# 64-byte places of two operands in a retention/GLA layer: sums of x in pairs, four of seven weight products shifted, a small tile ahead of the heads' output

## The chip, the core and the metric

The kernel runs on one core of a Trainium2 chip. TensorE (PE) multiplies, VectorE (DVE), ScalarE (ACT) and GpSimd (POOL) do the elementwise work, SyncE (SP) and POOL issue DMAs. The metric is the device time of one execution in microseconds; lower is better.

## The reference, cut to what matters

One layer with two branches over 512 positions and 16 meta positions, model width 1024:

```python
u = rms_norm(h, norm_gain)                       # (528, 1024)
(rq, rk, rv, rg, gq, gk, gv, gg, glr, m_ret, m_gla) = split(u @ w_in)
o_ret = head_group_norm(retention(rope(rq), rope(rk) / 16, rv)) * silu(rg)   # 4 heads, 256 -> 512
o_gla = head_rms_norm(gla(gq, gk, gv, log_sigmoid(glr @ w_gate_up + b_gate) / 16)) * silu(gg)
merged = sigmoid(m_ret) * (o_ret @ w_branch_ret) + sigmoid(m_gla) * (o_gla @ w_branch_gla)
out = rms_norm(h + merged @ w_out, final_norm_gain)[16:]
```

All is float32. The kernel splits each float32 operand into a rounded high part (hi) and the rest (lo), both float32r, and forms a product from three matmuls: hi x hi, hi x lo, lo x hi.

## The kernel before

Most of the time goes to `quad`, which multiplies x (two halves of 256 positions, th, by two halves of 512 rows, kh) by a block of 512 weight columns with seven block products in place of eight. The products are numbered 1, 2, 6, 7, 5, 4, 3 in the order they run. Products 1, 2 and 4 take a block of x itself (the names A11, A12 for the first half of positions, A22 for the second); 5, 6, 7 and 3 take sums of blocks, S1, S2, S3, S4, that `form` makes once. A list `fh` holds the seven high parts and `fl` the seven low parts. One product has 24 matmuls: two column halves t, four row blocks kk, and the three of hi and lo.

- In quads with `rows=True` (gg, gv, rg, rv) the weights' 256 columns stream as the moving operand and 128 positions of x are the stationary one. In mr, mg, rqk and gqk it is the other way round: 128 weight columns are stationary, and x's 256 or 264 positions stream.
- bg and wo1 use `quad` too, with lists of their own in place of fh and fl (`forms`).
- `wsplit` gives the tiles for hi and lo of the next weights (three buffers each); ScalarE casts to hi and VectorE subtracts for lo (`split`, line 154). The matmuls of the quads are line 318.
- `branch` and `ret_branches` multiply a head's turned output oh, ol (four row blocks by 512 positions, moving) by w_branch_ret (stationary, 128 columns), with `mm3` (lines 189 to 193); this is br. oh and ol of heads 0 to 2 are in the pool rp, those of head 3 take the place of x in the pool cp.

The order on each engine follows the code, with a pin that keeps the matmuls of a product together. `weave` mixes the quads with the chains of attention and gates. Weights come by SP's DMAs; the sums of two weight blocks come by DMAs from POOL that accumulate (line 282).

A tile's place in SBUF is a byte address within each partition, the same for all partitions. From the built program's memory map, modulo 128 bytes, before the change:

| operand | step from row block to row block | place modulo 128 |
|---|---|---|
| x, first half (A11, A12) | 2 x 272 x 4 = 2176 = 17 x 128 | 64 |
| x, second half (A22) | 2176 | 64 + 1088 = 0 |
| S1 to S4, one tile each, `[P, 4, 272]` | 272 x 4 = 1088 = 8.5 x 128 | 64, 0, 64, 0 |
| weights hi, lo, all products | 256 x 4 = 1024 | 64 |
| oh, ol of heads 0 to 2 | 2048 | 0 |
| oh, ol of head 3 | 2048 | 64 |

Of the kernel before, what the change touches and what calls it, by code (L numbers as in the profile page):

```python
# [21 lines left out]
F32 = mybir.dt.float32  # L22
F32R = mybir.dt.float32r
# [5 lines left out]
P = 128  # L29
D = 1024  # L30
T = 512
NM = 16
# [14 lines left out]
SOFF = (0, 512, 896, 1152)  # L47
E_U, E_D, E_A, E_B, E_END, E_ND = range(6)
A11, A12, A22, S1, S2, S3, S4 = range(7)


def constants():
# [56 lines left out]
def hybrid_kernel(ctx: ExitStack, tc: tile.TileContext, I, out: bass.AP):  # L109
# [22 lines left out]
    al = {(th, kh): xl[kh][:, :, th] for th in range(2) for kh in range(2)}  # L132
    fh = [ah[0, 0], ah[0, 1], ah[1, 1]]
    fl = [al[0, 0], al[0, 1], al[1, 1]]
    fh += [cp.tile([P, 4, HW], F32R, tag=f"fh{i}", name=f"fh{i}") for i in range(3, 7)]
    fl += [cp.tile([P, 4, HW], F32R, tag=f"fl{i}", name=f"fl{i}") for i in range(3, 7)]

    rt = cp.tile([P, NTB + 1], F32, name="rt")
    rneg = cp.tile([P, NTB + 1], F32, name="rneg")
    rb = cp.tile([P, 2, HT], F32, name="rb")  # L140
    um = cp.tile([P, KD, 32], F32, name="um")
    sel = cp.tile([P, P], F32R, name="sel")
    rgain = cp.tile([P, 16], F32, name="rgain")
    ggain = cp.tile([P, 8], F32, name="ggain")
# [50 lines left out]
            order[:] = [m]  # L195

    def rstd_of(x, n, rows, name, eps=EPS):
        v = sp.tile([P, 1], F32, tag="rv", name=f"{name}_v")
        r = sp.tile([P, 1], F32, tag="rr", name=f"{name}_r")
        nc.vector.tensor_scalar(v[:rows], x, 1.0 / n, eps, op0=ALU.mult, op1=ALU.add)  # L200
        R["pow"] = nc.gpsimd.tensor_tensor(r[:rows], v[:rows], mhalf[:rows], op=ALU.pow)
        return r
# [45 lines left out]
    def wraw(name, shape=(P, 4, 256)):  # L248
        return wp.tile(list(shape), F32, tag="raw", name=name, bufs=6)

    def wsplit(shape, name):
        return (wp.tile(shape, F32R, tag="whi", name=f"{name}_h", bufs=3),
                wp.tile(shape, F32R, tag="wlo", name=f"{name}_l", bufs=3))

    low = []

    def quad(cols, rows, name, evac, meta=None, adds=True, ahead=False, behind=None, src=None,
# [42 lines left out]
            return form[kk // 2][:, kk % 2] if isinstance(form, list) else form[:, kk]  # L300

        def prepare(i, w):
            hi, lo = wsplit([P, 4, 256], f"{name}_{i}")
            low[:] = split(hi, lo, w)
            return hi, lo

# [33 lines left out]
        if meta is not None:  # L340
            psm = pat(f"{name}_pm")
            for n in range(2):
                for kh in range(2):
                    for g in range(4):
                        nc.tensor.matmul(psm[32 * g:32 * g + 32, n * 256:(n + 1) * 256], um[:, 4 * kh + g, :],
                                         (w11, w21)[kh][:, g, :] if n == 0 else (w12, w22)[kh][:, g, :], start=n == 0 and kh == 0, stop=kh == 1,
                                         skip_group_check=n > 0)
        product(1, A11, w11, b, True)
# [223 lines left out]
    wps = pat("warm_p")  # L572
    for _ in range(10):
        nc.tensor.matmul(wps, wzero[:, :P], wzero, start=True, stop=True)
    nc.gpsimd.memset(um, 0.0)
    nc.gpsimd.tensor_copy(sel, selr)
    nc.gpsimd.memset(ones, 1.0)

# [9 lines left out]
    def small_rows():  # L588

        for k in range(KD):  # L590
            g = k % 4
            m = nc.tensor.matmul(psm[32 * g:32 * g + 32], um[:, k, :], graw[k // 2][:, k % 2, :],
                                 start=k < 4, stop=k >= 4)
            if k == 0:
                pin(m)
        for s in range(2):
            for k in range(KD):
                g = k % 4
                m = nc.tensor.matmul(glr[s][32 * g:32 * g + 32, :HT], wl[:, k, :], u[k // 4][:, k % 4, s],
                                     start=k < 4, stop=k >= 4)  # L600
        order[:] = [m]

    for q in range(4):
        raw = graw[q]
        hi, lo = wsplit([P, 2, 512], f"gv0_{q}")
        for kk in range(2):
            kh, k = divmod(2 * q + kk, 4)
            g = ng[:, 2 * q + kk:2 * q + kk + 1]
            cast = nc.scalar.activation(xh[kh][:, k, :, :HT], u[kh][:, k], AF.Copy, scale=g)
            casts.append(cast)  # L610
            if k == kh == 0:
                nc.vector.tensor_copy(hi[:, kk, :], raw[:, kk, :])
                w = nc.vector.tensor_sub(lo[:, kk, :], raw[:, kk, :], hi[:, kk, :].bitcast(F32))
            x = nc.vector.scalar_tensor_tensor(xl[kh][:, k, :, :HT], u[kh][:, k], g, xh[kh][:, k, :, :HT].bitcast(F32),
                                               op0=ALU.mult, op1=ALU.subtract)
            if k == kh == 0:
                after(x, w)
            if k or kh:
                split(hi[:, kk, :], lo[:, kk, :], raw[:, kk, :])

        if q == 3:
            for kh in range(2):
                for k in range(4):
                    x = nc.scalar.activation(u[kh][:, k], u[kh][:, k], AF.Copy, scale=ng[:, 4 * kh + k:4 * kh + k + 1])
                    if kh == 1:
                        act(x)
                    else:
                        after(x, casts[-1])
                x = nc.vector.tensor_copy(um[:, 4 * kh:4 * kh + 4, :NM].rearrange("p k (h m) -> p k h m", h=2),
                                          u[kh][:, :, :, 256:HT])  # L630
                if kh == 1:
                    vec(x)
            small_rows()
        steps = [(t, kk, j) for t in range(NTB) for kk in range(2) for j in range(3)]
        if q < 3:
            steps.sort(key=(lambda x: (x[1], -x[2] % 3 if x[1] == 0 else x[2])) if q < 2 else (lambda x: x[1]))
        for t, kk, j in steps:
            kh, k = divmod(2 * q + kk, 4)
            c = slice((t % 2) * P, (t % 2 + 1) * P)
            m = nc.tensor.matmul(pss[t], (al if j == 1 else ah)[t // 2, kh][:, k, c], (lo if j == 2 else hi)[:, kk, :],  # L640
                                 start=q == kk == j == 0, stop=q == 3 and kk == 1 and j == 2)
            pin(m)
            order[:] = [m]
# [241 lines left out]
    def gla_attention(p):  # L885
# [14 lines left out]
        def decays(b):  # L900
            lah, lal = split_la(b, P)
            for h in range(2):
# [11 lines left out]
                G["exp"] = nc.scalar.activation(X[:, 2:5, :], pf[:, :384].rearrange("p (e t) -> p e t", e=3), AF.Exp)  # L914
                Q[b, h] = gp.tile([P, 4, P], F32, tag="gQ", name=f"gQ{n}", bufs=4)
                K[b, h] = gp.tile([P, 4, P], F32, tag="gK", name=f"gK{n}", bufs=2)
                TO[b, h] = sp.tile([P, 1], F32, tag="gto", name=f"gto{n}")
                qb = q[:, h, b * P:(b + 1) * P].unsqueeze(1).to_broadcast([P, 4, P])
                kb = k[:, h, b // 2, (b % 2) * P:(b % 2 + 1) * P].unsqueeze(1).to_broadcast([P, 4, P])
                nc.vector.tensor_mul(K[b, h], X[:, 2:6, :], kb)  # L920
# [405 lines left out]
    def ret_attention(h):  # L1326
        sh, sl, sm = R["s", h]
        vh, vl = R["v", h]
        vm, sg = R["vm", h], R["sg", h]

        oh, ol = [(rp if h < 3 else cp).tile([P, 4, T], F32R, tag=f"o{n}" if h < 3 else f"x{n}0", name=f"o{n}{h}")
                  for n in "hl"]
        R["o", h] = oh, ol

        def values(ib):
            ps = pat(f"av{h}{ib}")
            for jb in range(ib + 1):
                o = SOFF[jb] + (ib - jb) * P
                mm3(ps, sh[:, o:o + P], sl[:, o:o + P], vh[:, jb, :], vl[:, jb, :], jb == 0, False)
            nc.tensor.matmul(ps, sm[:, ib * P:(ib + 1) * P], vm, start=False, stop=True)  # L1340
            b6 = sp.tile([P, 6], F32, tag="b6", name=f"b6{h}{ib}")
            mv = sp.tile([P, 2], F32, tag="mv", name=f"mv{h}{ib}")
            nc.vector.bn_stats(b6, ps)
            nc.vector.bn_aggr(mv, b6)
            r = rstd_of(mv[:, 1:2], 1.0, P, f"g{h}{ib}")
            nm = sp.tile([P, 1], F32, tag="nm", name=f"nm{h}{ib}")
            nc.vector.scalar_tensor_tensor(nm, mv[:, 0:1], -1.0, r, op0=ALU.mult, op1=ALU.mult)  # L1347
            on = tmp(f"on{h}{ib}")
            nc.scalar.activation(on, ps, AF.Identity, scale=r, bias=nm)  # L1349
            nc.vector.tensor_mul(sg[:, ib, :], on, sg[:, ib, :])  # L1350

        for ib in range(NTB):
            values(ib)
            R["pow", h] = R["pow"]
            yield
        if h < 2:
            yield
        for half in range(2):
            turn(sg, half, oh, ol, rgain, h * 4, f"ot{h}")
            yield  # L1360
# [82 lines left out]
    for h in range(4):  # L1443
# [10 lines left out]
        else:  # L1454
# [2 lines left out]

    mh, ml = [[cp.tile([P, 4, T], F32R, tag=f"x{n}1", name=f"m{n}0"),
               rp.tile([P, 4, T], F32R, tag=("sg", "vl")[n == "l"], name=f"m{n}1")] for n in "hl"]
    sums = [[cp.tile([P, 4, 256], F32R, tag=f"f{n}{i}", name=f"ms{n}{i}") for i in range(3, 7)] for n in "hl"]  # L1460
    mforms = [[m[0][:, :, :256], m[1][:, :, :256], m[1][:, :, 256:], *x] for m, x in zip((mh, ml), sums)]

    def merged(k, t):
# [43 lines left out]
    def square(t, o):  # L1507
# [4 lines left out]
        if o == 768:  # L1512
            nc.vector.tensor_tensor_reduce(sq[:, :256], hh, hh, 1.0 / D, vs[t], ALU.mult, ALU.add, v)
        else:
            ss = sp.tile([P, 1], F32, tag="ss", name=f"fss{t}{o}")
            nc.scalar.activation(sq[:, :256], hh, AF.Square, accum_out=ss)
            nc.gpsimd.tensor_scalar(v, ss, 1.0 / D, vs.get(t, EPS), op0=ALU.mult, op1=ALU.add)
        vs[t] = v
# [1 line left out]
            nc.gpsimd.tensor_mul(hh, hh, fgb[:, o:o + 256])  # L1520
        if o < 768:
            return
        r = sp.tile([P, 1], F32, tag="rr", name=f"fr{t}")
        nc.gpsimd.tensor_tensor(r, v, mhalf, op=ALU.pow)
        h0, h1 = hs[0][:, t, :], hs[1][:, t, :]
        nc.scalar.activation(h0, h0, AF.Copy, scale=r)
# [82 lines left out]
```

## Time and profile before

| | |
|---|---|
| time, median of 3 runs | 761.6 us (761.6 to 762.16) |
| profiled execution | 761.8 us, of it the span 760.0 us |
| TensorE busy | 749.8 us (99%), 5595 matmuls |
| VectorE busy | 611.4 us (80%) |
| ScalarE busy | 450.8 us (59%) |
| GpSimd busy | 141.9 us (19%) |
| granted TensorE clock, mean over the span | 0.997 |
| DMA | 116.89 MB, mean 154 GB/s |

A matmul's record runs from its start to the modelled end of its way through the array, so neighbours overlap; how long a matmul holds the array is seen from start to start, or from a group that spans many of them. In the view by stretches a row gives the stretch, its length, then for PE, PEld, DVE, ACT and POOL the busy time and the count of instructions in it, then the granted clock, the DMA share and GB/s. In the chain a row gives start, length and what ran. In the timeline a row gives start, length, engine, line, operation, out<-in, shape and count, and in brackets idle time ahead of it.

### The profile page before, as it was taken

To read this page: it belongs to the slowest core of one execution; us is meant where nothing else is said; L and a number is where in the kernel's file an instruction comes from. 1 tells how busy PE (TensorE), PEld (TensorE's weight loads), DVE (VectorE), ACT (ScalarE), POOL (GpSimd) and SP (SyncE) were. 2 spreads that over 40 slices of the span, in tenths; PEclk is the share of its full clock that TensorE was granted. 3 is DMA by queue.
4 is the path that set the end of the run, shared out by engine and by line. 5 is a ranking of instruction groups with operands and counts; after the bars stand their busy time and mean duration, and the time that the engine had idled before them with its cause. 6 is when DMAs were issued, how large, how long until landed. Compare 5 with 4: busy or idle time off the path is not lost.

```text
span 760.0 us, 14059 instructions
## 1 busy us (share of the span) xinstructions
PE 749.8 (99%) x5595; PEld 701.8 (92%) x5595; DVE 611.4 (80%) x873; ACT 450.8 (59%) x764; POOL 141.9 (19%) x172
## 2 busy tenths in 40 slices
PE   9999999999989999999999999999999999999996
PEld 6799899999989999999989999989999999988996
DVE  6799878689897789789957688966787989775994
ACT  7897584666974566546546555646464756532562
POOL 2211200112231122110530100440011210111142
PEclk9999999999999999999999999999999999999999
DMA  9864321822568972733783562794476356687503
GB/s 301 287 138 100 95 85 43 184 82 65 145 157 232 303 170 88 173 111 130 200 245 119 120 158 86 203 238 119 131 165 144 109 141 193 229 191 201 131 29 112
DMA packets 99994, 116.89 MB, mean 154 GB/s; under 512 B 5716, under 2 KB 90836, under 8 KB 99672
## 3 DMA queue, kind: packets, MB, share of 16 engines
q1 hardware_dynamic: 79896, 88.19, 36.7%
q0 software_dynamic: 19744, 27.27, 19.7%
q8 instruction: 44, 0.72, 0.4%
q10 hardware_dynamic: 288, 0.53, 0.2%
q14 instruction: 22, 0.18, 0.1%
HBM read 104.44 MB, written 11.53 MB: 153 GB/s over the span
## 4 chain that ended last, share of the span: by engine, by line
PE 91%; DVE 6%; issue 2%; ACT 1%; POOL 0%; POOLq 0%; DVEq 0%
PE rqk_b L318 6%; PE rv_b L318 6%; PE rg_b L318 6%; PE rqk_c L318 5%; PE br_p L189 4%; PE br_p L193 4%; PE br_p L192 4%; PE gg_b L318 3%; PE mr_b L318 3%; PE mg_b L318 3%; PE gv_p L640 3%; PE rv_c L318 3%; PE bg_b L318 3%; PE rg_c L318 3%; PE gg_c L318 2%
## 5 line engine op out<-in xcount | busy, mean ns | idle before, releaser
L189 PE MATMUL br_p<-oh,br_h 128*128 128x512 f32 x128 | 50.4, 394 | 0.0
L192 PE MATMUL br_p<-ol,br_h 128*128 128x512 f32 x128 | 50.4, 393 | 0.0
L193 PE MATMUL br_p<-oh,br_l 128*128 128x512 f32 x128 | 50.4, 393 | 0.0
L154 ACT CAST rv_h<-rv_w 128x1024 fp32r<-128x1024 f32 x24 | 25.3, 1052 | 27.1 <-DVE rv_w L371 9.6
L154 DVE TENSOR_TENSOR rv_l<-rv_w,rv_h 128x1024 fp32r<-128x1024 f32 x24 | 29.3, 1222 | 9.2 <-ACT rv_h L154 9.2
L154 DVE TENSOR_TENSOR rg_l<-rg_w,rg_h 128x1024 fp32r<-128x1024 f32 x20 | 24.4, 1222 | 8.7 <-ACT rg_h L154 8.7
L282 POOL DMA_DIRECT2D rqk_x<-in_w_in_dram x8 | 10.4, 1302 | 108.0 <-DVE rv_l L154 80.6
L154 ACT CAST rg_h<-rg_w 128x1024 fp32r<-128x1024 f32 x20 | 21.0, 1051 | 15.8 <-PE br_p L192 6.2
L193 PEld LDWEIGHTS br_p<-oh,br_l 128*128 128x128 f32 x128 | 24.0, 188 | 5.7
L189 PEld LDWEIGHTS br_p<-oh,br_h 128*128 128x128 f32 x128 | 24.0, 188 | 5.0
L192 PEld LDWEIGHTS br_p<-ol,br_h 128*128 128x128 f32 x128 | 24.0, 188 | 5.0
L154 ACT CAST br_h<-br_w 128x1024 fp32r<-128x1024 f32 x16 | 16.8, 1049 | 19.2 <-PE br_p L192 9.9
L154 ACT CAST rqk_h<-rqk_w 128x1024 fp32r<-128x1024 f32 x20 | 21.0, 1052 | 11.6 <-PE rqk_c L318 2.9
L1349 ACT ACTIVATE on<-av,nm,g_r 128x512 f32<-128x512 f32 x16 | 12.5, 780 | 25.4 <-DVE nm L1347 25.4
L318 PE MATMUL rv_b<-rv_l,fh 128*128 128x256 f32 x96 | 27.1, 282 | 0.2 <-DVE rv_l L154 0.2
L318 PE MATMUL rqk_b<-fh,rqk_h 128*128 128x256 f32 (+1 forms) x96 | 27.2, 283 | 0.0
L318 PE MATMUL rqk_b<-fh,rqk_l 128*128 128x256 f32 (+1 forms) x96 | 27.1, 283 | 0.0
L318 PE MATMUL rqk_b<-fl,rqk_h 128*128 128x256 f32 (+1 forms) x96 | 27.1, 282 | 0.0
L318 PE MATMUL rg_b<-rg_h,fl 128*128 128x256 f32 x96 | 27.0, 281 | 0.0
L154 DVE TENSOR_TENSOR rqk_l<-rqk_w,rqk_h 128x1024 fp32r<-128x1024 f32 x20 | 24.4, 1220 | 3.2 <-ACT rqk_h L154 3.2
L318 PE MATMUL rv_b<-rv_h,fl 128*128 128x256 f32 x96 | 27.0, 281 | 0.0
L318 PE MATMUL rg_b<-rg_h,fh 128*128 128x256 f32 x96 | 26.9, 281 | 0.0
(720 smaller groups left out, 3266.6 us busy)
## 6 DMA issues: line engine op xcount, KB each, us to landing
rv_w<-in_w_in_dram SPq DMA_DIRECT2D x16, 512.0 KB, 4.1
br_w<-in_w_branch_ret_dram SPq DMA_DIRECT2D x16, 512.0 KB, 3.4
rqk_w<-in_w_in_dram SPq DMA_DIRECT2D x12, 512.0 KB, 4.8
rg_w<-in_w_in_dram SPq DMA_DIRECT2D x12, 512.0 KB, 4.9
rqk_x<-in_w_in_dram SPq DMA_DIRECT2D x8, 512.0 KB, 3.9
rqk_x<-in_w_in_dram POOLq DMA_DIRECT2D x8, 512.0 KB, 8.2
rg_x<-in_w_in_dram SPq DMA_DIRECT2D x8, 512.0 KB, 3.7
rg_x<-in_w_in_dram POOLq DMA_DIRECT2D x8, 512.0 KB, 7.7
```

The source lines that it names most:

```text
L154: return nc.scalar.copy(hi, src), nc.vector.tensor_sub(lo, src, hi.bitcast(F32))
L189: m = nc.tensor.matmul(o, lh, rh, start=first, stop=False)
L192: nc.tensor.matmul(o, lh, rl, start=False, stop=False)
L193: m = nc.tensor.matmul(o, ll, rh, start=False, stop=last)
L282: x = nc.gpsimd.dma_start(t, block(0, 1), accum_op=ALU.add)
L318: m = nc.tensor.matmul(ps[t][:, :n] if wide else ps[t], l, r, start=first and j == 0, stop=kk == 3 and j == 2, skip_group_check=not fresh ...
L640: m = nc.tensor.matmul(pss[t], (al if j == 1 else ah)[t // 2, kh][:, k, c], (lo if j == 2 else hi)[:, kk, :], start=q == kk == j == 0, sto ...
L1349: nc.scalar.activation(on, ps, AF.Identity, scale=r, bias=nm)
```

## The change

1. S1 and S2 share one tile `[P, 4, 2, 272]` with row blocks interleaved, S3 and S4 another, so that a form's step from row block to row block is 2176, as in x. S1 and S3 then lie at 64, S2 and S4 at 0 modulo 128 for all kk. The sums in the output product (`sums`) use the same two tiles, as two `[P, 4, 256]` halves.
2. `wsplit` makes its tiles 32 elements (128 bytes) longer, so that the three buffers lie 4224 bytes apart. With `odd` the weights start 64 bytes into the tile; otherwise 0 or 128 bytes, by turns that follow the buffers' rotation. `odd` is set for products 1, 2, 5 and 7 of the quads on fh.
3. A memset of a 64-byte tile, `gap`, on POOL ahead of head 0's oh: oh and ol of heads 0 to 2 move from 0 to 64 modulo 128.
4. Room for it: statistics tiles (rv, rr, gto, b6, mv, nm, ss) have 3 or 4 buffers in place of 5, and um (x of the meta positions) is one tile of 160 columns in which eight windows of 32 columns overlap by 16. The second 16 columns of a window, zero before, now hold the next block's values; they reach rows of a sum that nothing reads.

With it, the reads of a matmul's moving operand and of the stationary operand that is loaded beside it lie 64 bytes apart modulo 128 in all products of the 20 quads on fh (products 1 and 2 before: 0; product 4: 64; the S products: 0 and 64 by turns). For br of heads 0 to 2 it goes from 64 to 0. Modulo 256, hi and lo of the odd products lie 128 bytes apart; in the others, at one place, except where buffers don't come in turn (72 of the 288 matmuls of br).

```diff
 A11, A12, A22, S1, S2, S3, S4 = range(7)
+ODD = (1, 2, 5, 7)
...
-    fh += [cp.tile([P, 4, HW], F32R, tag=f"fh{i}", name=f"fh{i}") for i in range(3, 7)]
-    fl += [cp.tile([P, 4, HW], F32R, tag=f"fl{i}", name=f"fl{i}") for i in range(3, 7)]
+    for n, f in (("h", fh), ("l", fl)):
+        for i in range(2):
+            t = cp.tile([P, 4, 2, HW], F32R, tag=f"f{n}{i}", name=f"f{n}{i}")
+            f += [t[:, :, 0], t[:, :, 1]]
...
-    um = cp.tile([P, KD, 32], F32, name="um")
+    ums = cp.tile([P, 160], F32, name="um")
+    um = [ums[:, k * NM:k * NM + 32] for k in range(KD)]
...
-        v = sp.tile([P, 1], F32, tag="rv", name=f"{name}_v")
-        r = sp.tile([P, 1], F32, tag="rr", name=f"{name}_r")
+        v = sp.tile([P, 1], F32, tag="rv", name=f"{name}_v", bufs=3)
+        r = sp.tile([P, 1], F32, tag="rr", name=f"{name}_r", bufs=4)
...
-    def wsplit(shape, name):
-        return (wp.tile(shape, F32R, tag="whi", name=f"{name}_h", bufs=3),
-                wp.tile(shape, F32R, tag="wlo", name=f"{name}_l", bufs=3))
+    turn_of = [0]
+
+    def wsplit(shape, name, odd=False):
+        n, b = int(np.prod(shape[1:])), turn_of[0] % 3
+        turn_of[0] += 1
+        x = []
+        for t in ("hi", "lo"):
+            o = 16 if odd else 32 * ((b + (t == "hi")) % 2)
+            x.append(wp.tile([P, 32 + 1024], F32R, tag=f"w{t}", name=f"{name}_{t[0]}", bufs=3)[:, o:o + n])
+        return [t.rearrange("p (k c) -> p k c", k=shape[1]) if len(shape) > 2 else t for t in x]
...
-            hi, lo = wsplit([P, 4, 256], f"{name}_{i}")
+            hi, lo = wsplit([P, 4, 256], f"{name}_{i}", forms[0] is fh and i in ODD)
...
+        if h == 0:
+            nc.gpsimd.memset(rp.tile([P, 16], F32, name="gap"), 0.0)
         oh, ol = [(rp if h < 3 else cp).tile([P, 4, T], F32R, tag=f"o{n}" if h < 3 else f"x{n}0", name=f"o{n}{h}")
...
-    sums = [[cp.tile([P, 4, 256], F32R, tag=f"f{n}{i}", name=f"ms{n}{i}") for i in range(3, 7)] for n in "hl"]
+    sums = [[t[:, j] for i in range(2) for t in [cp.tile([P, 2, 4, 256], F32R, tag=f"f{n}{i}", name=f"ms{n}{i}")] for j in range(2)]
+            for n in "hl"]
```

The instructions and their order are the same on PE, ACT, DVE and SP. On POOL one is added. Before, POOL has there, between the sums for rqk0 (keys and queries of head 0) and those for rg0 (its gates):

```order
L282 DMA rqk_x_3141<-in_w_in_dram 128x4x256
L282 DMA rqk_x_3142<-in_w_in_dram 128x4x256
L1201 MEMSET km 128x256
L282 DMA rg_x_3373<-in_w_in_dram 128x4x256
L282 DMA rg_x_3374<-in_w_in_dram 128x4x256
```

and after, with the lines of the changed program:

```order
L293 DMA rqk_x_3137<-in_w_in_dram 128x4x256
L293 DMA rqk_x_3138<-in_w_in_dram 128x4x256
L1212 MEMSET km 128x256
L1343 MEMSET gap 128x16
L293 DMA rg_x_3369<-in_w_in_dram 128x4x256
L293 DMA rg_x_3370<-in_w_in_dram 128x4x256
```

The memset of gap stands between the memset of km and the DMA that adds into rg0's third weight block, and waits for the last matmuls on what lay in its place.

More of the change, by code (lines that the diff above doesn't have):

```diff
@@ L344, in quad @@
                     for g in range(4):
-                        nc.tensor.matmul(psm[32 * g:32 * g + 32, n * 256:(n + 1) * 256], um[:, 4 * kh + g, :],
+                        nc.tensor.matmul(psm[32 * g:32 * g + 32, n * 256:(n + 1) * 256], um[4 * kh + g],
                                          (w11, w21)[kh][:, g, :] if n == 0 else (w12, w22)[kh][:, g, :], start=n == 0 and kh == 0, stop=kh == 1,
@@ L574, in hybrid_kernel @@
         nc.tensor.matmul(wps, wzero[:, :P], wzero, start=True, stop=True)
-    nc.gpsimd.memset(um, 0.0)
+    nc.gpsimd.memset(ums, 0.0)
     nc.gpsimd.tensor_copy(sel, selr)
@@ L591, in small_rows @@
             g = k % 4
-            m = nc.tensor.matmul(psm[32 * g:32 * g + 32], um[:, k, :], graw[k // 2][:, k % 2, :],
+            m = nc.tensor.matmul(psm[32 * g:32 * g + 32], um[k], graw[k // 2][:, k % 2, :],
                                  start=k < 4, stop=k >= 4)
@@ L628, in hybrid_kernel @@
                         after(x, casts[-1])
-                x = nc.vector.tensor_copy(um[:, 4 * kh:4 * kh + 4, :NM].rearrange("p k (h m) -> p k h m", h=2),
+                x = nc.vector.tensor_copy(ums[:, 4 * kh * NM:(4 * kh + 4) * NM].rearrange("p (k h m) -> p k h m", k=4, h=2),
                                           u[kh][:, :, :, 256:HT])
@@ L916, in decays @@
                 K[b, h] = gp.tile([P, 4, P], F32, tag="gK", name=f"gK{n}", bufs=2)
-                TO[b, h] = sp.tile([P, 1], F32, tag="gto", name=f"gto{n}")
+                TO[b, h] = sp.tile([P, 1], F32, tag="gto", name=f"gto{n}", bufs=4)
                 qb = q[:, h, b * P:(b + 1) * P].unsqueeze(1).to_broadcast([P, 4, P])
@@ L1340, in values @@
             nc.tensor.matmul(ps, sm[:, ib * P:(ib + 1) * P], vm, start=False, stop=True)
-            b6 = sp.tile([P, 6], F32, tag="b6", name=f"b6{h}{ib}")
-            mv = sp.tile([P, 2], F32, tag="mv", name=f"mv{h}{ib}")
+            b6 = sp.tile([P, 6], F32, tag="b6", name=f"b6{h}{ib}", bufs=3)
+            mv = sp.tile([P, 2], F32, tag="mv", name=f"mv{h}{ib}", bufs=3)
             nc.vector.bn_stats(b6, ps)
@@ L1345, in values @@
             r = rstd_of(mv[:, 1:2], 1.0, P, f"g{h}{ib}")
-            nm = sp.tile([P, 1], F32, tag="nm", name=f"nm{h}{ib}")
+            nm = sp.tile([P, 1], F32, tag="nm", name=f"nm{h}{ib}", bufs=3)
             nc.vector.scalar_tensor_tensor(nm, mv[:, 0:1], -1.0, r, op0=ALU.mult, op1=ALU.mult)
@@ L1514, in square @@
         else:
-            ss = sp.tile([P, 1], F32, tag="ss", name=f"fss{t}{o}")
+            ss = sp.tile([P, 1], F32, tag="ss", name=f"fss{t}{o}", bufs=3)
             nc.scalar.activation(sq[:, :256], hh, AF.Square, accum_out=ss)
@@ L1522, in square @@
             return
-        r = sp.tile([P, 1], F32, tag="rr", name=f"fr{t}")
+        r = sp.tile([P, 1], F32, tag="rr", name=f"fr{t}", bufs=4)
         nc.gpsimd.tensor_tensor(r, v, mhalf, op=ALU.pow)
```

## The prediction

> **What bounds the kernel now.** I read the page first (busy time, then the chain that ended last), then the chain in order of time, then stretches of the span cut to single stages, and last the waits of TensorE.
>
> ```profile
> span 760.0 us, 14059 instructions
> PE 749.8 (99%) x5595; PEld 701.8 (92%) x5595; DVE 611.4 (80%) x873; ACT 450.8 (59%) x764; POOL 141.9 (19%) x172
> PE 91%; DVE 6%; issue 2%; ACT 1%; POOL 0%; POOLq 0%; DVEq 0%
> ```
>
> TensorE is busy for 749.8 of 760.0 us and holds 91% of the chain, so a shorter kernel needs shorter matmuls, not fewer waits. Whether matmuls of one shape take the same time everywhere is the question, and it is answered by how often one starts.
>
> ```profile
> 209.85 0.28 PE L318 MATMUL mr_b<-fh,mr_l 128*128 128x256 f32 x1
> 209.85 0.19 PEld L318 LDWEIGHTS mr_b<-fh,mr_h 128*128 128x128 f32 x1
> 209.97 0.28 PE L318 MATMUL mr_b<-fh,mr_h 128*128 128x256 f32 x1
> ```
>
> A matmul starts 0.12 us after the last, though one is drawn 0.28 us long. The stationary operand of the next one is loaded during the first part of the running one (both rows start at 209.85). So two reads run side by side: the moving operand of matmul i and the stationary operand of matmul i+1. The change moves addresses of exactly these two. In the chain, 24 matmuls of one product are one piece; the pieces of one quad (rg0; order of products 1, 2, 6, 7, 5, 4, 3) are
>
> ```profile
> 275.26 2.85 PE rg_b L318 x24
> 278.11 2.85 PE rg_a L318 x24
> 280.96 2.83 PE rg_b L318 x24
> 283.80 2.84 PE rg_c L318 x24
> 286.64 2.84 PE rg_b L318 x24
> 289.48 2.75 PE rg_c L318 x24
> 292.23 2.85 PE rg_b L318 x24
> ```
>
> Six of seven need 2.83 to 2.85 us, product 4 (A22) needs 2.75: 114.6 ns a matmul against 118.8. Shape, code and the rotating weight buffers are the same; what differs is the addresses: x's second half of rows lies 64 bytes off the weights modulo 128, while in products 1 and 2 both lie on the same place modulo 128 and in products 3, 5, 6, 7 the distance alternates from k to k. The quads whose moving operand is x show a smaller step (mg: product 2, then product 4; rqk, 264 wide: 2, 4, and the 256-wide 5):
>
> ```profile
> 354.75 2.85 PE mg_a L318 x24
> 377.25 2.80 PE mg_c L318 x24
> ...
> 257.94 2.92 PE rqk_c L318 x24
> 269.52 2.90 PE rqk_c L318 x24
> 266.67 2.85 PE rqk_b L318 x24
> ```
>
> For the 512-wide matmuls of br the sign turns round. Of the four stretches below, each of 48 matmuls, heads 2, 3, 2, 3 in turn, head 2's oh lies 64 bytes off the weights and head 3's (in cp) on the same place:
>
> ```profile
> 666.28:677.49 11.21, 11.21 (x51) 8.98 (x50) 9.00 (x10) 2.86 (x4) 3.53 (x4) 1.00 0.73 144
> 677.49:688.39 10.90, 10.90 (x50) 9.01 (x49) 7.71 (x11) 3.97 (x5) 0.00 (x0) 1.00 1.04 274
> 688.39:699.59 11.20, 11.20 (x50) 8.98 (x49) 4.87 (x6) 2.72 (x3) 1.30 (x1) 1.00 0.64 155
> 699.59:710.49 10.90, 10.90 (x50) 9.01 (x49) 8.44 (x12) 4.21 (x6) 1.29 (x1) 1.00 0.94 244
> ```
>
> 11.20 against 10.90 us: 233.3 and 227.1 ns a matmul. So the distance matters, and which distance is good depends on the width.
>
> **The change, part by part.** After it, products 1, 2, 5 and 7 (the odd table) have weights moved by 64 bytes, and S1/S3 and S2/S4 lie with one distance for all k; every product of the 20 quads on fh has 64 bytes between the two reads. The gap tile puts oh and ol of heads 0 to 2 on the same place as the weights of br.
>
> - Row quads (gg0, gg1, gv1, rg0-3, rv0-3: 11). Products 6 and 3 get the very pattern of product 4 (hi and lo at one place modulo 256), so I give them all of it: 2.83 + 2.85 - 2 x 2.75 = 0.18 us a quad. Products 1, 2, 7, 5 get 64 bytes too, but their hi and lo lie 128 bytes apart, which no product of before has. Ends: nothing, and the whole step of 2 x 0.10 + 2 x 0.09 = 0.38. The nearest row is mg's 2.80, where a 64-byte distance in another order gives half the step; I take half, 0.19. 0.37 x 11 = 4.1 us (ends 2.0 and 6.2).
> - Quads with x moving, 256 wide (mr0, mr1, mg0, mg1): 0.05 for products 1 and 2, about 0.02 for each of the four S products; odd ones again at half: 0.11 x 4 = 0.4 us (0.2 to 0.7).
> - rqk0-3 and gqk1: 264 wide 2.92 to 2.90, their 256-wide products 2.85 to 2.80: 0.08 a quad with the odd at half, 0.4 us in all (0.2 to 0.65).
> - br of heads 0 to 2: 288 matmuls, six stretches of 48 at 0.31 us: 1.86 us. By the addresses 72 of them keep a 128-byte distance, for which I count half: 1.6 us (1.4 to 1.9).
> - Fewer statistics buffers, each write waiting for a reader three or four uses back. The shortest of these is at the tail: the Square at 743.88 will need that the POOL step which began at 742.27 and lasted 0.50 is done, 1.1 us earlier. Cost nothing; if POOL were late, at most that step's 0.5 us.
>
> ```profile
> 742.27 0.50 POOL L1517 TENSOR_SCALAR fv<-fss,fv 128x1 f32<-128x1 f32 x1 [1.73 <-ACT fsq L1516]
> 743.88 0.40 ACT L1516 ACTIVATE fsq<-hs 128x256 f32<-128x256 f32 x1
> ```
>
> - The gap memset stands on POOL behind the memset of km and ahead of rg0's accumulating DMA; it needs the matmuls of bg_c to be done (by 252.3), and POOL has nothing until 263.26, so 11 us cover it.
>
> ```profile
> 249.46 2.83 PE bg_c L318 x24
> ...
> 249.88 0.87 POOL L1201 MEMSET km<- 128x256 f32 x1
> 263.26 1.29 POOL L282 DMA_DIRECT2D rg_x<-in_w_in_dram  x1 [12.51 <-DVE rqk_l L154]
> ```
>
> - um smaller, copied as 64 elements in place of 4 x 16, and overlapping windows: one memset and two copies at the start, under loads; 32-column matmuls unchanged in number. Nothing.
> - S1/S2 in one tile: no row waits anew for the other half, since the same orders stand on every engine. Nothing.
>
> Gross: 4.1 + 0.4 + 0.4 + 1.6 = 6.5 us.
>
> **What of it is given back.** PE is not alone on the path in two places.
>
> ```profile
> PE bg_b L318 <- DVE bg_l L154: 1.3, 1, 1.3
> PE bg_b L318 <- ACT bg_x L334: 0.8, 1, 0.8
> 218.67 1.22 DVE L154 TENSOR_TENSOR bg_l<-bg_w,bg_h 128x1024 fp32r<-128x1024 f32 x1
> 219.80 3.43 DVE L154 TENSOR_TENSOR gs<-og,gs 128x1024 fp32r<-128x1024 f32 x1
> 218.84 3.30 POOL L1115 TENSOR_TENSOR og1gq<-og1gq,og 128x1024 f32<-128x1024 f32 x1
> 200.00:220.00 20.00, 19.97 (x172) 19.77 (x170) 18.21 (x20) 16.47 (x29) 6.74 (x7) 1.00 0.65 175
> 220.00:240.00 20.00, 17.94 (x138) 17.54 (x137) 17.13 (x16) 10.69 (x14) 3.46 (x2) 0.91 0.85 205
> ```
>
> At 222 to 225 PE waits 2.1 us for VectorE, whose gs took 3.43 us where such a step takes 1.2, with POOL's 3.30 us beside it; behind the wait the granted clock is 0.91 of the stretch, 0.09 x 20 = 1.8 us of it lost. The gains ahead of it are three row quads, gqk1 and mr0: 3 x 0.37 + 0.08 + 0.11 = 1.3 us. VectorE's work there follows PE only in part (it is busy 18.21 of 20 us ahead of it), so I count two thirds as given back: 0.9 us (0 to 1.3). The Trainium skill (SBUF — State Buffer, Who interferes with whom) says that a VectorE step with two SBUF inputs contends with a GpSimd step that reads SBUF; these two rows agree, and by it the 2.2 us stay wherever the two meet.
>
> ```profile
> 600.00:620.00 20.00, 19.81 (x182) 18.49 (x181) 19.97 (x26) 13.01 (x22) 0.57 (x1) 1.00 0.34 106
> ```
>
> Here VectorE is full, and PE waits for rv_l at 617. What rg3 and two products of rv3 gain ahead of it, 0.37 + 0.10 = 0.5 us, is given back. Net: 6.5 - 0.9 - 0.5 = 5.1 us. The profiled execution took 761.8 us (span 760.0 and 1.8 around it), the median of three is 761.6; 761.6 - 5.1 = 756.5 us.
>
> **The rivals.**
> 1. The odd products take the whole step too: 6.2 + 0.7 + 0.65 + 1.9 = 9.4, less 0.7 at 617 and 0.9 at 222: 7.8 us, 753.8 us (752.9 where VectorE follows PE). For it: bg, whose x lies 64 bytes off its weights in some products, has pieces below even rg's 2.75.
>
> ```profile
> 244.02 2.72 PE bg_a L318 x24
> ```
>
> Against: mg's half step. Chance 0.17.
> 2. The odd products take nothing: 2.0 + 0.2 + 0.2 + 1.4, less 0.7 in the two places: 3.1 us, 758.5 us. Chance 0.12.
> 3. The longer wait at 222 (2.1 us growing to over 3) costs a second stretch of halved clock, 1.8 us: 758.3 us. Chance 0.07.
> 4. The distance does nothing and the steps above come from other things. The Trainium skill (TensorE: Matmul & The Clock Gate, Step-by-step: what each phase is for) has two independent read ports, so that loading the next weights takes no bandwidth from the running matmul; by that rule no address matters here. As a mechanism of this kernel: product 4 and head 3 are quick for their place in the order, and the time stays 761.6 us. The trace speaks against it: 10.90 and 11.20 us alternate four times with nothing else changed. Chance 0.03.
> 5. Slower: the odd products land in a worse order of reads than before. The trace has none with hi and lo 128 bytes apart, and 64 bytes were bad for br, so a loss isn't excluded. There are 20 x 4 = 80 such products; the sure parts give 3.1 us, so they would have to lose 0.04 us each to cancel that and 0.06 each (2.84 to 2.90) to be 1.5 us slower, 763.1. The slowest 256-wide product of a quad that doesn't wait is
>
> ```profile
> 739.76 2.88 PE wo_b L318 x24
> ```
>
> so it asks for more than the worst row. Chance 0.03.
>
> **How the numbers follow.** The forecast has 0.58. Faster by over 0.2% (1.5 us, about what a measurement of this kernel tells from no change) are it and rivals 1, 2 and 3 except for a rest of 0.03: 0.91. Rival 4 and a part of that rest: 0.05; slower 0.04. The range goes from rival 1's better end (752.5) to rivals 2 and 3 falling together on the upper side (3.1 - 1.8 = 1.3 us, 760.3; 759.8 leaves out the last bit), with some 0.15 outside.
>
> **What the changed profile would show.** Right: the pieces of rg and rv at 2.75 to 2.80 in all seven products, products 6 and 3 nearest to product 4; the br stretches of head 2 at 10.9; a wait for bg_l at 221 longer than 1.3; a wait for rv_l at 612 longer than 0.2. Wrong: products 1, 2, 5, 7 at 2.84 or more; product 4 itself slower; br unchanged; a splitting step (1.22 us on VectorE, 1.05 on ScalarE) that grew; POOL's DMAs of rg0 later than the memset ahead of them allows.

## The result, and the profile after

The changed kernel takes 756.17 us (median of 5 runs, 755.76 to 756.25) against 761.72 us (5 runs, 761.6 to 762.16) for the kernel before, measured beside it: ratio 0.9926, 95% interval 0.9914 to 0.9937. The forecast was 756.5 us. The profiled execution took 755.93 us. Page of the kernel after: span, busy time, chain.

```profile
span 754.2 us, 14063 instructions
PE 743.4 (99%) x5595; PEld 696.1 (92%) x5595; DVE 610.3 (81%) x873; ACT 449.9 (60%) x764; POOL 142.1 (19%) x173
PE 91%; DVE 6%; issue 2%; ACT 1%; POOL 0%; POOLq 0%; DVEq 0%; ACTq 0%
```

The same matmuls, on PE for 6.4 us less; PE is the bound as before. The pieces of rg0 in the chain after, in the order of products 1, 2, 6, 7, 5, 4, 3:

```profile
273.36 2.79 PE rg_b L329 x24
276.15 2.82 PE rg_a L329 x24
278.97 2.73 PE rg_b L329 x24
281.70 2.81 PE rg_c L329 x24
284.50 2.82 PE rg_b L329 x24
287.32 2.73 PE rg_c L329 x24
290.05 2.72 PE rg_b L329 x24
```

Products 6 and 3 (third and last) have come down to product 4; 1, 2, 7 and 5 stop about halfway. The four stretches of br (heads 2, 3, 2, 3), cut at the same matmuls as before:

```profile
661.13:672.02 10.89, 10.89 (x51) 9.02 (x50) 8.91 (x10) 2.86 (x4) 3.52 (x4) 1.00 0.75 151
672.02:682.90 10.88, 10.88 (x50) 9.01 (x49) 7.72 (x11) 3.96 (x5) 0.00 (x0) 1.00 1.05 276
682.90:693.79 10.89, 10.89 (x50) 9.02 (x49) 4.85 (x6) 2.73 (x4) 1.31 (x1) 1.00 0.67 153
693.79:704.65 10.86, 10.86 (x50) 8.99 (x48) 8.43 (x12) 4.20 (x6) 1.28 (x1) 1.00 0.96 257
```

The alternation of 11.2 and 10.9 is gone. The places where PE waits, and the stretches around them:

```profile
PE bg_b L329 <- DVE bg_l L158: 1.3, 1, 1.3
PE bg_b L329 <- ACT bg_x L345: 0.6, 1, 0.6
PE rv_b L329 <- DVE rv_l L158: 0.4, 1, 0.4
PE rg_c L329 <- DVE rg_l L158: 0.3, 1, 0.3
```

```profile
220.00:240.00 20.00, 17.95 (x149) 17.35 (x148) 18.27 (x17) 10.06 (x13) 2.94 (x2) 1.00 0.90 217
580.00:600.00 20.00, 19.70 (x170) 19.49 (x169) 20.00 (x31) 13.85 (x23) 4.36 (x4) 1.00 0.41 102
600.00:620.00 20.00, 19.58 (x177) 18.05 (x176) 18.06 (x22) 10.12 (x17) 1.86 (x2) 1.00 0.47 137
```

The wait for bg_l at 222 us did not grow, and the clock of that stretch is 1.00 where it was 0.91. Just ahead of 600 us there is a new wait, for rg_l, and VectorE is busy all the time from 580 to 600 us. Before, it was not:

```profile
580.00:600.00 20.00, 20.00 (x171) 20.00 (x171) 18.69 (x32) 11.85 (x19) 6.24 (x6) 1.00 0.41 97
```

To see more than rg0, I took from the traces the time from one matmul's start to the next over the 264 matmuls that each product has in the 11 row quads (longer than 160 ns, a wait, left out). The last three kernels are experiments below.

| ns a matmul, product | 1 | 2 | 5 | 7 | 6 | 3 | 4 |
|---|---|---|---|---|---|---|---|
| before | 118.8 | 118.9 | 118.0 | 118.3 | 118.4 | 118.3 | 114.3 |
| after | 116.9 | 117.0 | 117.1 | 117.0 | 114.8 | 113.7 | 114.7 |
| no_odd | 118.8 | 118.8 | 118.9 | 118.9 | 114.7 | 113.7 | 114.9 |
| all_odd | 117.1 | 117.0 | 117.1 | 116.9 | 117.9 | 118.8 | 118.2 |
| aligned | 114.4 | 114.5 | 114.2 | 114.5 | 114.7 | 113.7 | 115.1 |

### The profile page after: what moved, and what is told of

It is laid out like the page before. It is cut to its first block, busy times and chain, and to the rows that moved or that the text cites. A ratio compares the mean times of both kernels' runs of the same rounds, so it can differ in the third digit from the quotient of the medians.

```text
span 754.2 us, 14063 instructions
## 1 busy us (share of the span) xinstructions
PE 743.4 (99%) x5595; PEld 696.1 (92%) x5595; DVE 610.3 (81%) x873; ACT 449.9 (60%) x764; POOL 142.1 (19%) x173
## 4 chain that ended last, share of the span: by engine, by line
PE 91%; DVE 6%; issue 2%; ACT 1%; POOL 0%; POOLq 0%; DVEq 0%; ACTq 0%
PE rqk_b L329 6%; PE rv_b L329 6%; PE rg_b L329 6%; PE rqk_c L329 5%; PE br_p L197 4%; PE br_p L196 4%; PE br_p L193 4%; PE gg_b L329 3%; PE mr_b L329 3%; PE gv_p L651 3%; PE mg_b L329 3%; PE rv_c L329 3%; PE rg_c L329 3%; PE bg_b L329 2%; PE gg_c L329 2%
## 5 line engine op out<-in xcount | busy, mean ns | idle before, releaser
L205 POOL TENSOR_TENSOR g_r<-g_v,mhalf 128x1 f32<-128x1 f32 x16 | 9.8, 612 | 90.8 <-DVE g_v L204 90.8
L329 PE MATMUL rg_b<-rg_l,fh 128*128 128x256 f32 x96 | 26.7, 278 | 0.0
L329 PE MATMUL rv_b<-rv_h,fh 128*128 128x256 f32 x96 | 26.6, 278 | 0.0
```

The source lines that it names most:

```text
L329: m = nc.tensor.matmul(ps[t][:, :n] if wide else ps[t], l, r, start=first and j == 0, stop=kk == 3 and j == 2, skip_group_check=not fresh ...
```

## The experiments

Two ideas stood against each other throughout: that the distance between the two reads sets a matmul's pace, and that something else in the change does (the place in the order, the moved instructions, tiles of another size). Beside the experiments the kernel before took 761.63 to 761.8 us, so their medians are compared directly.

**The gap tile alone** (gap_only), in the kernel before:

```diff
+        if h == 0:
+            nc.gpsimd.memset(rp.tile([P, 16], F32, name="gap"), 0.0)
         oh, ol = [(rp if h < 3 else cp).tile(
```

> The kernel before with the 64-byte gap tile ahead of oh and ol alone; weights, block sums and statistics buffers as before. Theory (the place of the two reads): only br of heads 0 to 2 changes, by what the changed kernel showed there, 1.5 us: 760.2 us (759.8 to 760.4), the br stretches of head 2 at 10.9 us and those of heads 0 and 1 some 0.1 to 0.35 us a head shorter, the row quads at 2.83 to 2.85 as before. Rival (place does nothing, br gained from something else in the change): 761.7 us, head 2 at 11.2.

760.2 us, ratio 0.9984 (0.9975 to 0.9992). The first two stretches of br, heads 2 and 3:

```profile
665.65:676.58 10.93, 10.93 (x51) 9.02 (x50) 8.95 (x10) 2.87 (x4) 3.52 (x4) 1.00 0.73 148
676.58:687.46 10.88, 10.88 (x50) 9.01 (x49) 7.71 (x11) 3.97 (x5) 0.00 (x0) 1.00 1.04 274
```

Head 2 went from 11.21 to 10.93 us. All of br gained 1.6 us, the row quads nothing. 64 bytes ahead of a tile, with the same instructions on PE, are worth this much. One thing was not expected: mg0 and mg1, whose operands kept their addresses, took 0.3 us more (see the last section).

**The odd table empty** (no_odd), in the kernel after:

```diff
-ODD = (1, 2, 5, 7)
+ODD = ()
```

> The changed kernel with an empty odd table: the sums stay in pairs, the gap tile and the weights of 4224 bytes stay, but the weights of products 1, 2, 5 and 7 are not moved by 64 bytes, so that they lie on the same place modulo 128 as what they are read beside. Theory: in the row quads these four go back from 117.0 to about 118.8 ns a matmul (the value of products 1 and 2 before), products 6, 3 and 4 stay at 114 to 115: 11 x 4 x 24 x 1.8 ns = 1.9 us, and 0.3 to 0.6 more in the quads with x moving: 758.4 us (758.0 to 758.9), or 760.1 if the stretch of halved clock at 226 us returns with it. Rival (the 64 bytes of the odd table are worth nothing, the gain is the pairs' alone): 756.2 us.

758.58 us, ratio 0.9962 (0.995 to 0.9975): 2.4 us more than with the table. Products 1, 2, 5 and 7 are at 118.8 to 118.9 ns, while 6 and 3 keep their gain (table): pairing the sums pays for 6 and 3 alone, the odd table for the others.

**All seven products odd** (all_odd), in the kernel after:

```diff
-ODD = (1, 2, 5, 7)
+ODD = (1, 2, 3, 4, 5, 6, 7)
```

> The changed kernel with all seven products in the odd table: products 3, 4 and 6, which lay 64 bytes off what they are read beside, are moved by 64 bytes too and so come back onto its place modulo 128. Theory (it is the distance that counts, not the moving): in the row quads these three go from 113.7 to 114.8 ns a matmul up to 118 to 119, 264 x 3 x 4.4 ns = 3.5 us, with 0.1 to 0.3 in the other quads: 759.8 us (759.2 to 760.4); products 1, 2, 5, 7 stay at 117.0. Rival (tiles that begin off a multiple of 128 bytes are read faster, whatever lies beside them): 756.2 us or less.

759.72 us, ratio 0.9975 (0.9966 to 0.9985), 3.6 us more than after. The last four pieces of rg0 (products 7, 5, 4, 3):

```profile
283.32 2.80 PE rg_c L329 x24
286.11 2.82 PE rg_b L329 x24
288.93 2.99 PE rg_c L329 x24
291.92 2.87 PE rg_b L329 x24
```

Product 4, the fastest before, is now slow (2.99 holds a short wait besides; 118.2 ns over all row quads), with the same shift that made products 7 and 5 faster. So what counts is where the two reads lie to each other, not the shift by itself.

**hi and lo of the odd products on one place** (aligned), in the kernel after:

```diff
-            o = 16 if odd else 32 * ((b + (t == "hi")) % 2)
+            o = 16 if odd else 32 * ((b + 1) % 2)
+            if t == "lo" and turn_of[0] == 1:
+                wp.tile([P, 32], F32, name="between")
```

and two buffers in place of three for rv, b6, mv and nm, which pays for the 128 bytes and keeps everything behind them on its address.

> The changed kernel with 128 bytes between the hi and the lo weight buffers, so that hi and lo of an odd product lie on one place modulo 256 too, as those of an even one do (four statistics tiles have two buffers in place of three to pay for it). Each odd product of a row quad then has word for word the pattern of distances of product 4. Theory (what kept the odd products at half a step is hi and lo lying 128 bytes apart): their matmuls go from 117.0 to 113.5 to 114.6 ns, 11 x 4 x 24 x 2.9 ns = 3.1 us, less 0.2 in the quads with x moving (116.1 to 116.7 ns); some 0.7 is given back at 222 and at 610 us: 754.0 us (753.3 to 754.6), or 755.7 if the longer wait at 222 us brings back a stretch of halved clock. Rival (an odd product is slower for its place in the quad or for which half of x it reads, not for hi and lo): 117.0 ns stay, 756.2 us.

754.11 us, ratio 0.99 (0.9886 to 0.9913). Products 1, 2, 6 and 7 of rg0:

```profile
272.86 2.72 PE rg_b L331 x24
275.58 2.77 PE rg_a L331 x24
278.35 2.75 PE rg_b L331 x24
281.10 2.75 PE rg_c L331 x24
```

All four odd products run at 114.2 to 114.5 ns. What had kept them at half the step is that hi and lo lay 128 bytes apart, although every single distance was 64 modulo 128 in both kernels. So 128 bytes are not the whole period; the pattern modulo 256 counts too. It does not help everywhere: in mg0, where x moves, the same four products went from 116.1 to 116.4 ns in after to 117.5 to 117.9 here.

**The small edits alone** (small): the kernel before with the packed um and the fewer statistics buffers, and two unused tiles that keep all other addresses.

> The kernel before with the packed um and the fewer statistics buffers alone, with two unused tiles that keep every other address where it was. Theory: nothing, 761.7 us (761.4 to 762.0). Rival (a write that waits for a reader three uses back delays somebody): up to 0.5 us more, 762.2.

762.13 us, ratio 1.0007 (0.9998 to 1.0016). The median lies above the theory's range and at the rival's 762.2, and the interval, which reaches to 1.2 us more, can't tell the two apart. The trace speaks for the theory: it shows no wait for a statistics tile. The profile is 0.8 us longer than that of before. Of this, 0.5 us lie at the start (see the halved clock, below), and 0.3 us of PE at 167.7 us go back to VectorE, which waited 2.66 us (1.58 in the profile before) for a DMA that no edit touches:

```profile
164.44 1.23 DVE L358 TENSOR_TENSOR mr_x<-mr_w,mr_w 128x1024 f32<-128x1024 f32 x1 [2.66 <-DMA mr_w<-in_w_in_dram]
```

**The slow gs** (relief): in the kernel after, GpSimd's step beside it goes to VectorE.

```diff
-        nc.gpsimd.tensor_add(a01, a01, a00)
         yield
...
         gform(A22, a11, list(low))
+        nc.vector.tensor_add(a01, a01, a00)
         yield
```

> The changed kernel with one step moved: the sum of og1gq and og for S4 is made by VectorE after ga22l in place of GpSimd beside gs. Theory (gs takes 3.43 us because GpSimd's 3.2 us step runs beside it, and PE's wait at 222 us hangs on it): gs takes 1.2 us, the wait of 2.3 us shrinks to a few tenths, and the 1.2 us of the moved step on VectorE are covered: 754.0 us (753.7 to 754.8). Rival (gs is slow for another reason): gs stays at 3.4 us and the moved step's 1.2 us come on top: 756.2 to 757.4 us.

754.95 us, ratio 0.9911 (0.9898 to 0.9925), a little above the range of the theory. First the two steps in the kernel after, then gs in this one, its stretch, and what PE waits for:

```profile
219.28 3.43 DVE L158 TENSOR_TENSOR gs<-og,gs 128x1024 fp32r<-128x1024 f32 x1
218.43 3.20 POOL L1126 TENSOR_TENSOR og1gq<-og1gq,og 128x1024 f32<-128x1024 f32 x1
```

```profile
218.86 1.22 DVE L158 TENSOR_TENSOR gs<-og,gs 128x1024 fp32r<-128x1024 f32 x1
```

```profile
220.00:240.00 20.00, 19.07 (x160) 18.47 (x159) 18.21 (x19) 10.68 (x13) 1.30 (x1) 1.00 0.91 233
```

```profile
PE bg_c L329 <- ACT bg_x L345: 0.5, 1, 0.5
PE bg_c L329 <- DVE bg_l L158: 0.3, 1, 0.3
```

gs took 1.22 us as soon as GpSimd's step was gone: the 2.2 us were contention. The Trainium skill (SBUF — State Buffer, Who interferes with whom) names exactly this pair, a VectorE step with two SBUF inputs and a GpSimd step that reads SBUF; this run agrees. PE gained 1.25 us by its matmuls' starts and not 2.2, since the moved step takes 1.22 us of VectorE just ahead of the splitting of product 4's weights, and there PE waits next.

**A longer wait** (stall_more), in the kernel after, ahead of the sum of bg0's weights:

```diff
+            if name == "bg0":
+                nc.vector.tensor_copy(w21, w21)
             nc.vector.tensor_add(w21, w21, w11)
```

> The changed kernel with one more step on VectorE ahead of the sum of bg's weights at 222 us, a copy of 1024 elements in place (0.6 to 1.2 us), so that PE waits 2.8 us and that much longer. Theory (the clock is halved for a stretch of 3.4 us where PE stood idle for more than about half of the stretch ahead of it, and the grid of these stretches falls differently in each run, so that the kernels so far had it in some runs): the halved stretch comes in every run and costs 1.1 us net beside the added step: 757.9 to 758.5 us. Rival (a wait costs its own length alone): 756.8 to 757.4 us.

758.58 us, ratio 0.9958 (0.9945 to 0.9972), just above the theory's range. The copy took 0.68 us, and the order on VectorE changed with it: the split of S4's form (1.21 us) and two steps of 0.68 us came ahead of product 4's split. So the wait grew by more than the copy, and a median above the rival's 756.8 to 757.4 us does not by itself speak against the rival. The halved clock is there too: by the matmuls' starts PE lost 3.0 us between 215 and 232. The halved stretch has 19 matmuls where some 29 fit, which makes 1.1 to 1.2 us of it the clock's and the rest, 1.8 to 1.9 us, waiting. The trace records the granted clock in stretches of 3.413 us, whose grid lies differently against the kernel in each execution. Cut at that grid, the stretch that holds most of the wait and the one behind it (in the columns PE busy and clock) in before, small and stall_more:

```profile
223.07:226.48 3.41, 1.43 (x10) 1.23 (x11) 3.41 (x5) 2.72 (x5) 0.00 (x0) 1.00 0.26 75
226.48:229.89 3.41, 3.41 (x19) 3.41 (x18) 3.09 (x4) 1.19 (x3) 0.00 (x0) 0.50 0.83 242
```

```profile
224.02:227.43 3.41, 1.56 (x11) 1.35 (x12) 3.41 (x5) 2.72 (x5) 0.00 (x0) 1.00 0.29 77
227.43:230.85 3.42, 3.42 (x19) 3.42 (x18) 3.15 (x5) 1.33 (x3) 0.00 (x0) 0.50 0.81 258
```

```profile
226.79:230.20 3.41, 1.49 (x10) 1.11 (x9) 3.41 (x6) 2.04 (x3) 0.00 (x0) 1.00 0.75 246
230.20:233.62 3.42, 3.42 (x19) 3.42 (x18) 2.00 (x2) 0.00 (x0) 1.31 (x1) 0.50 0.86 248
```

and in aligned and gap_only:

```profile
220.44:223.85 3.41, 1.89 (x15) 1.49 (x13) 3.41 (x3) 2.13 (x3) 0.56 (x1) 1.00 0.65 102
223.85:227.27 3.42, 2.78 (x22) 2.58 (x22) 3.42 (x6) 2.46 (x5) 0.00 (x0) 1.00 0.69 217
```

```profile
222.14:225.55 3.41, 2.73 (x21) 2.32 (x20) 3.41 (x3) 1.53 (x2) 1.19 (x1) 1.00 0.73 117
225.55:228.97 3.42, 2.23 (x19) 2.23 (x20) 3.42 (x6) 2.52 (x3) 0.00 (x0) 1.00 0.54 167
```

gap_only has the wait of the kernel before, and loses no clock: its grid cuts the wait in two. In the twelve profiles of this study the clock halves after each stretch in which PE was busy for 1.56 us or less (four of them) and after none with 1.89 us or more around this wait. At the end of the span it is the same: 1.47 us in gap_only halved the next stretch, 1.65 in small and 1.84 in before did not. That the longer wait brings the halved stretch in every execution, as expected, did not hold. One halved stretch takes 0.002 of the mean clock (0.5 x 3.41 of 757 us). Of the four executions of stall_more one has a mean clock of 0.999, so it had none; it took 758.12 us, the others 758.57 to 758.66.

**Both gains in one kernel**: the edits of aligned, and relief's step one stage later (best):

> Both changes that gained, in one kernel: hi and lo of the odd products on one place (128 bytes between the buffers), and the sum for S4 on VectorE in place of GpSimd, this time one stage later, behind the splitting of product 4's weights, for which PE waited in the run with the moved step (its 1.25 us of 2.2). Theory: the 1.3 us of that run and some 0.8 us of its rest of waits: 754.1 - 2.1 = 752.0 us (751.5 to 752.8). Rival (VectorE is the bound of that stage, 16.7 of 17.0 us busy, wherever the step stands): 754.1 - 1.2 = 752.9 us.

756.64 us, ratio 0.9936 (0.9924 to 0.9948), 2.5 us slower than aligned alone. Both the theory and its rival missed. Its longest wait of PE, and a piece of its chain:

```profile
PE bg_b L331 <- DVE gs L1139: 2.5, 1, 2.5
```

```profile
231.23 7.21 PE bg_b L331 x47
```

One stage later on VectorE put S4's own split, which needs the sum, behind two more splits of weights; PE waited 2.5 us for it, and the 47 matmuls behind took 7.21 us where 47 take 5.6: a halved stretch lies there.

**Both gains, the step where relief had it** (align_relief), **and wo1's weights moved too** (align_relief_wo):

```diff
-            hi, lo = wsplit([P, 4, 256], f"{name}_{i}", forms[0] is fh and i in ODD)
+            hi, lo = wsplit([P, 4, 256], f"{name}_{i}", i in ODD if forms[0] is fh else name == "wo1" and i not in (2, 4))
```

> The kernel with hi and lo on one place, and the sum for S4 on VectorE where it stood in the first run with the moved step (ahead of the splitting of product 4's weights, S4's own split three steps behind it). In the run where it stood one stage later, S4's split came three VectorE steps later still, PE waited 2.5 us for it, and the clock was halved behind that. Theory: the two gains add up, 754.1 - 1.25 = 752.9 us (752.4 to 753.6), with a wait of 1 to 1.5 us left between 222 and 227 us. Rival (PE arrives 0.6 us earlier than in that run, and VectorE, which is the bound there, gives none of it): 753.5 us.

> The same, and five products of the last quad, wo1, with their weights moved: for products 1, 6, 7 and 3 the distance modulo 256 from what PE moves to the next weights goes from 0 to 192 for all 24 matmuls, for product 5 from 0 to 64. Theory (the distance alone sets the pace): 119.8 ns a matmul go to 113.4 in four products, as in bg's product 2, and to 118 in the fifth: 4 x 24 x 6.4 + 24 x 1.8 ns = 0.65 us less than the run beside it, 752.2 us. Rival (wo1 is slow for its operands' own place or its place in the order): no difference.

753.1 us, ratio 0.9886 (0.9869 to 0.9902), and 752.55 us, ratio 0.9884 (0.9869 to 0.9898). By the matmuls' starts the moved step gives 1.26 us on top of aligned, as in relief. Product 3 of wo1, the last, first without and then with the shift:

```profile
732.04 2.88 PE wo_b L331 x24
```

```profile
730.63 2.73 PE wo_b L331 x24
```

It came down by 0.15 us, the step of 6.4 ns a matmul that was expected. But the whole quad gave 0.2 us, not 0.65: the other shifted products wait for VectorE's splits of wo1's weights and sums, which take the gain. The medians of these two can't be told apart. Both beat the kernel before and the kernel after.

## Why the prediction was right, step by step

- **Products 6 and 3, the full step:** 2.0 us expected, 0.9 + 1.2 = 2.1 measured (264 x 3.5 and 264 x 4.6 ns).
- **Products 1, 2, 5, 7, half a step:** 2.1 expected, 1.6 measured. The half was taken from mg's smaller step, by analogy, and that it came near is luck: mg's pattern has hi and lo at one place. aligned showed the cause in the row quads, hi and lo 128 bytes apart. With it the odd products take the whole step, as in rival 1, and the 754.1 us are near the 753.8 that rival 1 named.
- **Product 4** was to stay; it lost 0.1 us. A slower product 4 was named as a sign of being wrong, and the odd pieces of rg0, at 2.79 to 2.82 us, end a little above the 2.80 that was named as right; both are small beside the gain.
- **mr and mg; rqk and gqk1:** 0.4 + 0.4 expected, 0.6 + 0.5 measured.
- **br:** 1.6 expected, 1.5 measured. The 72 matmuls with 128 bytes between the reads gained little, not half; of two neighbouring pieces of 12 of them in head 1 the first has that distance (2.80 before):

```profile
500.08:502.88 2.80, 2.80 (x15) 2.26 (x14) 2.28 (x3) 1.62 (x3) 2.42 (x3) 1.00 1.10 346
502.88:505.63 2.75, 2.75 (x13) 2.25 (x12) 2.72 (x4) 1.50 (x2) 1.63 (x2) 1.00 1.22 243
```

- **Gross:** 6.5 expected, 6.1 measured.
- **Given back at 222 us:** 0.9 expected, 0.1 measured. This step failed. gap_only, which has no gain ahead of that place, and after, which came there with 1.1 us gained, differ by 0.1 us in the stretch from 215 to 232. VectorE's steps there came earlier with PE's (gs by 0.52 us, from 219.80 to 219.28, PE's first matmul of bg0 by 0.6): the 18.21 of 20 us busy ahead of the wait, from which the two thirds were taken, was work that followed PE.
- **Given back around 610 us:** 0.5 expected, 0.6 measured, but most of it one step earlier, at rg_l (0.45 us of PE's time at rg3), because VectorE is now full from 580 on (20.00 of 20, 18.69 before).
- **Nothing** for buffers and um: small's trace agrees, but its time alone would allow up to 1.2 us. The memset of gap ran at 251.68 us in gap_only, 12 us ahead of rg0's DMA (264.12).
- **The halved clock** was read as the price of a wait's length (rival 3). It depends on how the wait falls on the grid. The profile before had such a stretch, the profile after had none, and that is 1.2 us between the two profiles that the change did not make; the other way, PE's first matmuls run at half pace (427 ns a warm-up matmul in place of 213) until the grid's first full stretch, which came 1.0 us later in the profile after, and the start took 0.5 us longer. Between the two profiles this leaves 5.4 + 1.2 - 0.5 = 6.1 against 5.9, 0.2 us that I could not place. By the medians, 6.1 - 0.1 - 0.6 = 5.4 us stand against 761.72 - 756.17 = 5.55. That the grid averages out of them is not shown: all five executions of the changed kernel have a mean clock of 0.999, so none of them had a halved stretch.

The right total is thus partly luck: a gross 0.4 too high and 0.8 too much given back cancel. Rival 4, two read ports that don't know of each other, fell with all_odd: the place of three products' weights alone moved 3.6 us.

## What to carry to other kernels

Where PE is busy nearly all the time, compare groups of equal matmuls by the time from start to start; if they differ by 2 to 4%, look at where the moving operand of one and the stationary operand of the next lie modulo 256, for hi and lo apart, and test it with a filler tile of 64 bytes, which leaves PE's instructions as they are. The good distance depends on the width (here 192 for 256 columns, 0 for 512), so measure it for each shape, and over many products, since one stream can run at two paces with the same addresses. Such a gain is kept only as far as the engine that feeds PE can follow, and moving a step to relieve that engine also moves what depends on it.

## What was not expected of the hardware

- 256-wide matmuls: the distance of a moving read from the next stationary read, modulo 256, always 192 mostly gives 113.3 to 114.2 ns (bg1's products 2, 5 and 6), always 64 about 118 (bg1's product 4), always 0 119.8 (wo1), always 128 about 119 to 120 (bg's product 1). 512-wide: 0 gives 226.7 (up to 230.6 in two pieces of gap_only), 192 gives 233.3, 128 about 232.
- The same six distances in turn (three of 192, three of 64) give 114.4 ns or 117.0 ns, depending on which matmul the turn begins with. Why is open.
- The distance alone does not fix the pace. bg0's product 2 has 192 for all its matmuls and the same addresses in after and in relief, yet 15 matmuls (from the first row to the second) take 1.77 us in after (shown first) and 1.70 in relief, 118.0 and 113.3 ns each:

```profile
220.38 0.40 PE L329 MATMUL bg_a<-ga,bg_h 128*128 128x256 f32 x2
222.15 0.40 PE L329 MATMUL bg_a<-ga,bg_h 128*128 128x256 f32 x2
```

```profile
219.50 0.39 PE L329 MATMUL bg_a<-ga,bg_h 128*128 128x256 f32 x2
221.20 0.39 PE L329 MATMUL bg_a<-ga,bg_h 128*128 128x256 f32 x2
```

In the same way mg0's products 3, 5 and 7 took 116.8 to 117.0 ns before and 118.4 to 118.5 in gap_only. What sets the pace besides the distance is open; in the row quads it does not hide the effect, since each product's pace in the table is a mean over 11 quads and returns within 0.8 ns wherever its pattern of distances returns.
- The Trainium skill (TensorE: Matmul & The Clock Gate, What's actually happening) has a free-running window of about 3.4 us and the half clock after an idle window. The grid of 3.413 us agrees; the window need not be idle: in small, 1.56 us busy of 3.41 halved the next one, 1.65 did not.
